# Rope queries of the second four heads made inside the second pair of attention heads, in a two-layer hybrid encoder on one core

## The chip, the cores and the metric

The kernel runs on one core of a Trainium2 chip. The metric is the device time of one execution in microseconds. The engines named below are TensorE (PE, with its weight loads as PEld), VectorE (DVE), ScalarE (ACT), GpSimd (POOL) and SyncE (SP). POOL and SP issue the transfers of this kernel, each in its own order.

## The reference

Two layers work on x, 512 positions by 2048. Each layer makes one wide projection of the normalised x, runs three groups of heads on parts of it, multiplies by a gate, projects back and adds the normalised result to x. The lines that matter here are those of the latent attention (8 heads; each query and key has 128 plain and 64 rotated components) and of the memory attention (4 heads against 256 memory tokens):

```python
q = (rmsnorm(q_lat, q_norm_g[l]) @ w_uq[l]).reshape(b, s, MLA_HEADS, QK_HEAD_DIM)
q = jnp.concatenate([q[..., :QK_NOPE_DIM],
                     apply_rope(q[..., QK_NOPE_DIM:], cos[:, :, None, :], sin[:, :, None, :])], axis=-1)
kv = (rmsnorm(kv_lat, kv_norm_g[l]) @ w_ukv[l]).reshape(b, s, MLA_HEADS, QK_NOPE_DIM + V_HEAD_DIM)
k_nope, v = kv[..., :QK_NOPE_DIM], kv[..., QK_NOPE_DIM:]
a_out = mla_attention(q, k, v)              # softmax(q k^T) v, 8 heads, 512 x 512
mem_n = rmsnorm(mem, mem_norm_g[l])
m_out = memory_attention(q_mem, mem_n, w_mk[l], w_mv[l])   # 4 heads, 512 x 256
y = jnp.concatenate([a_out, c_out, m_out], axis=-1) * jax.nn.silu(gate)
x = x + rmsnorm(y @ w_o[l], post_norm_g[l])
```

`apply_rope` multiplies the 64 components by a table of cosines and sines: with halves a and b it returns a·cos − b·sin and b·cos + a·sin. The queries of all eight heads need it. Here they are made in two halves: the first serves heads 0 to 3, the second heads 4 to 7.

## The kernel before

**Products.** Every fp32 product is three matmuls of a number split in two parts, high and low (`mm3`, lines 267 to 269). A split is a pair of instructions: ACT writes the high part, DVE the rest (`split_to`, lines 272 and 273). Weights come from memory as 128x1024 tiles `wr` in a pool of 8 raw tiles, and are split to `wh` (ACT, line 184) and `wl` (DVE, line 185), in pools of 3 tiles each. Larger things (queries Q, keys K, values V, transposed probabilities PT, the rotated queries QR, the split memory tokens mHL) lie in a pool of 19 slabs of 128x2048. The tile that takes over a slab or a raw tile waits until every reader of the old one is done, a transfer that reads it included.

**The attention part of a layer** is `mixer` (line 1202). It begins with a prelude: the products of the first half of the rope queries (`p0`, 24 matmuls into two PSUM tiles `qr`), the gates, the rotation of the first half, and the products of the second half (`p1`, 24 matmuls more). Then 16 steps follow for the four memory heads (one head, four blocks of 128 queries, scores of 128x256), so m = 16, and 32 steps for the eight latent heads, which are taken in four pairs (pair 0 is heads 0 and 1, steps m to m + 7; pair 1 is heads 2 and 3, steps m + 8 to m + 15). A step puts one block's scores `sc` on PE, and behind it the softmax: the negative row maximum `nm` on DVE (line 1125), the exponential and the scaling `P` on ACT (1128, 1131) with the reciprocal `rec` on DVE (1130). Some steps later the block's probabilities are transposed (`ptp`, line 1141) and split, and the head's output `o` is made from them and V. The scores of a latent head end in two matmuls of rotated parts (lines 1122 and 1123), which read the slab QR: heads 0 to 3 read the first half's, heads 4 to 7 the second half's.

**Work between the steps.** `between` is a table from the step's number to other work that is put behind that step's scores. It holds the steps that make Q, K and V of the next pair (`qkv_steps`, spread over the pair before), the rotation of the second half, and, in layer 0, eight steps that split the memory tokens for layer 1 (`mem_turned_steps`: ACT line 190, DVE line 191, into `mHL`, then transfers to `mTd` in memory by POOL).

**A rotation** has four steps. `first` is one DVE product of 128x1024 with the table `tab` (line 1013), `second` two of 128x512 (1017, 1018), `both` one difference and one sum of 128x512 (1022, 1023), and `away` splits the result into `qrh` and `rm` and writes both to memory with two transfers by POOL (line 1031). `fetch` then reads the result back into QR with four transfers of 256 KB by POOL (line 1036), in which each of four groups of 32 partitions takes one quarter: the first two quarters are the high parts, the last two the low parts.

**What sets the order.** PE, SP and POOL take their instructions in the order in which the program writes them. For DVE and ACT a scheduler chooses the order when the kernel is built, from the same program, and it moves work of the neighbouring steps past each other; on the chip each engine then goes strictly in its order.

Of the kernel before, what the change touches and what calls it, by code (L numbers as in the profile page):

```python
# [82 lines left out]
class Program:  # L83
# [22 lines left out]
    def add(self, fn, units=(), room=0.0, ahead=None):  # L106

        self.steps.append((list(units), fn, room, self.ahead if ahead is None else ahead))
# [114 lines left out]
def encoder(tc, x, xt, mem, memt, positions, columns, w_in, q_norm_g, w_uq, w_qr, kv_norm_g, w_ukv,  # L223
# [4 lines left out]
    depth = w_in.shape[0]  # L228
# [14 lines left out]
    pr = Program(nc, raw_p, hi_p, lo_p)  # L243
# [9 lines left out]
    def bank(name="ps", dt=F32):  # L253
        return banks.tile([P, 512], dt, tag="bank", name=nm(name))

    def slab(name, dt=F32):
        return slabs.tile([P, D], dt, tag="slab", name=nm(name))
# [7 lines left out]
    def mm3(ps, a, b, first, last, **kw):  # L265
        (ah, al), (bh, bl) = a, b
        nc.tensor.matmul(ps, ah, bh, start=first, stop=False, **kw)  # L267
        nc.tensor.matmul(ps, ah, bl, start=False, stop=False, **kw)  # L268
        nc.tensor.matmul(ps, al, bh, start=False, stop=last, **kw)  # L269

    def split_to(hi, lo, src):
        nc.scalar.copy(hi, src)
        nc.vector.tensor_tensor(lo, src, hi.bitcast(F32), op=ALU.subtract)
# [571 lines left out]
    def mem_turned_steps(l):  # L845
        st = {}

        def unit(q):
            def place():
                if q % 2 == 0:  # L850
                    st[q // 2] = slab("mHL", F32R)
                return tuple(st[q // 2][:, o:o + 512] for o in ((q % 2) * 512, 1024 + (q % 2) * 512))
            return Unit(("mT", l, q), {("mT", l, q): [memt[:, 2 * q:2 * q + 2, :]]}, alloc=place,
                        gain=lambda: [G[f"gm_{l}"][:, 2 * q + a:2 * q + a + 1] for a in range(2)])

        def step(q):
            def f(ops):
                if q % 2:
                    c = (q % 4 - 1) * 512
                    for i in range(2):  # L860
                        nc.gpsimd.dma_start(G["mTd"][2 * (q // 4) + i, :, c:c + 1024],
                                            st[q // 2][:, i * 1024:(i + 1) * 1024].bitcast(F32))
            return f
        return [(step(q), [unit(q)]) for q in range(8)]
# [177 lines left out]
    def qkv_steps(l, pair, st):  # L1042
        wl = w_uq[l].rearrange("(a p) (h c) -> p a h c", p=P, c=NOPE + ROPE)
        wkv = w_ukv[l].rearrange("(a p) c -> p a c", p=P)
        qk, kk = ("uq", l, pair), ("ukv", l, pair)
        qu = Unit(qk, {qk: [wl[:, :, 2 * pair + i, :NOPE] for i in range(2)]})
        ku = Unit(kk, {kk: [wkv[:, :, pair * 512:(pair + 1) * 512]]})

        def two(name):
            return slab(name, F32R).rearrange("p (s i c) -> p s i c", s=2, i=2)  # L1050

        def fq(i):
            def g(*ch):
                if ch:
                    st["qw"] = ch[0]
                    st["Q"] = two("Q")
                hi, lo = (a[:, i * 512:(i + 1) * 512].rearrange("p (j c) -> p j c", j=4) for a in st["qw"])
                cH, cL = G["cq"]
                ps = bank("qps")
                for j in range(4):  # L1060
                    mm3(ps, (hi[:, j, :], lo[:, j, :]), (cH[:, j, :], cL[:, j, :]), j == 0, j == 3)
                split_to(st["Q"][:, 0, i, :], st["Q"][:, 1, i, :], ps)
            return g

        def fk(i):
            def g(*ch):
                if ch:
                    st["kw"] = tuple(a.rearrange("p (j c) -> p j c", j=2) for a in ch[0])
                    st["K"] = two("K")
                hi, lo = st["kw"]  # L1070
                cH, cL = G["ckv"]
                ps = bank("kps")
                for j in range(2):
                    mm3(ps, (hi[:, j, i * 256:i * 256 + P], lo[:, j, i * 256:i * 256 + P]),
                        (cH[:, j, :], cL[:, j, :]), j == 0, j == 1)
                split_to(st["K"][:, 0, i, :], st["K"][:, 1, i, :], ps)
            return g

        def fv(b):
            def g():  # L1080
                if b == 0:
                    st["V"] = slab("V", F32R).rearrange("p (s k c) -> p s k c", s=2, k=NT)
                hi, lo = (a.rearrange("p j (h c) -> p j h c", h=2)[:, :, :, NOPE:] for a in st["kw"])
                cH, cL = G["ckv"]
                ps = bank("vps")
                for i in range(2):
                    sl = slice((2 * b + i) * P, (2 * b + i + 1) * P)
                    for j in range(2):
                        mm3(ps[:, i * 256:(i + 1) * 256].rearrange("p (h c) -> p h c", h=2),
                            (cH[:, j, sl], cL[:, j, sl]), (hi[:, j], lo[:, j]), j == 0, j == 1)  # L1090
                p3 = ps.rearrange("p (i c) -> p i c", i=2)
                split_to(st["V"][:, 0, 2 * b:2 * b + 2, :], st["V"][:, 1, 2 * b:2 * b + 2, :], p3)
            return g

        return [(fq(0), [qu]), (fq(1), []), (fk(0), [ku]), (fk(1), []), (fv(0), []), (fv(1), [])]
# [65 lines left out]
    def mla_head(h, st):  # L1161
        i = h % 2

        def src():
            Q, K, V = st["Q"], st["K"], st["V"]
            ds = slice(i * P, (i + 1) * P)
            return (Q[:, 0, i], Q[:, 1, i], K[:, 0, i], K[:, 1, i]), (lambda k: V[:, 0, k, ds], lambda k: V[:, 1, k, ds])
        return head_iters(h, h, src, S, h < HEADS - 1)

    def mem_head(i):  # L1170
        def src():
            Q, K, V = G["Qm"], G["Km"], G["Vm"]
            ds = slice(i * P, (i + 1) * P)
            return ((Q[0][:, i], Q[1][:, i], K[:, 0, i], K[:, 1, i]),
                    (lambda k: V[:, 0, k, ds], lambda k: V[:, 1, k, ds]))
        return head_iters(12 + i, None, src, MT)
# [18 lines left out]
    def spread(n, steps, start=0.0):  # L1195

        out = {}
        for k, s in enumerate(steps):
            out.setdefault(int(n * start + k * n * (1 - start) / len(steps)), []).append(s)
        return out  # L1200

    def mixer(l, C, gates, pair2, tail):

        add(tables_fetch)
        add(mem_fetch)
        gs = [(g, []) for g in gates]
        (p0, rotate0, fetch0), (p1, rotate1, fetch1) = (q_rope_steps(l, g) for g in range(2))
        put(p0[:1], gs[:4], p0[1:])
        put(rotate0, gs[4:], p1)
        sts = [{} for _ in range(4)]  # L1210
        qkv = qkv_steps(l, 0, sts[0])
        qkv[0] += (0.0, 1)
        qkv[2] += (0.0, 0)
        its = [it for i in range(4) for it in mem_head(i)]
        m = len(its)
        between = spread(m, qkv)
        between.setdefault(6, []).append((fetch0, []))
        for k, f in zip((2, 4, 6, m + 2), rotate1):
            between.setdefault(k, []).append(f)
        between.setdefault(m - 3, []).append((lambda: pr.prep_next(), []))  # L1220
        for pair in range(4):
            for i in range(2):
                its += mla_head(2 * pair + i, sts[pair])
            nxt = tail if pair == 3 else spread(6 if pair == 2 else 8, qkv_steps(l, pair + 1, sts[pair + 1]))
            if pair == 2:
                nxt.update(pair2)
            if pair < 2 and l + 1 < depth:
                turned = turned if pair else mem_turned_steps(l + 1)
                for k in range(4):
                    nxt.setdefault(2 * k + 1, []).append(turned[4 * pair + k])  # L1230
            for k, v in nxt.items():
                between.setdefault(m + 8 * pair + k, []).extend(v)
        between.setdefault(m + 9, []).append((fetch1, []))
        pipeline(its, between, m)


# [138 lines left out]
    def put(*passes):  # L1375
        for steps in passes:
            for s in steps:
                add(*s)
# [22 lines left out]
    for l in range(depth):  # L1401
        G["left"] = L = Left(l > 0)
        C, gs, owns = projection(l)
# [151 lines left out]
        if l + 1 < depth:  # L1555
            add(lambda: G.update(mTd=dram.tile([4, P, D], F32, name="mTd")))
        mixer(l, C, gates, {6: [(use_y, []), (low(0), [])], 7: [(low(1), [])]}, last_pair)
        add(sums(1))
        add(gains(0))
# [55 lines left out]
```

## Time and profile before

| | |
|---|---|
| median of 3 runs | 1482.05 us (1480.98 to 1482.29) |
| the profiled execution | 1483.54 us |
| its span, first to last instruction | 1481.8 us |
| busy PE, DVE, ACT, POOL | 99%, 73%, 58%, 18% |
| granted TensorE clock, mean | 0.998 |
| layer 0: prelude's end, memory heads, pair 0 | 447.4 to 453.0, to 478.0, to 507.3 us |
| layer 1: memory heads, pair 0, pair 1 | 1186.2 to 1211.0, to 1240.0, to 1269.0 us |

A row of a timeline gives the start, the length, the engine, the line, what is written and read, and in brackets the idle time before it and what ended it. A row of a window gives its length and then, for PE, PEld, DVE, ACT and POOL in this order, the busy time with the number of instructions, and at last the granted clock, the transfers' share and GB/s. Matmuls are pipelined: a 128x512 matmul has a row of 0.39 us, but in an unbroken run such matmuls start 0.227 us apart, so a pause that is shorter than the difference shows as no idle time.

### The profile page before, as it was taken

How to read it: one execution, taken by the hardware profiler on the slowest of the kernel's cores; microseconds unless marked ns; L12 is line 12 of the kernel's file. 1: busy time of each engine (PE TensorE's matmuls, PEld its weight loads, DVE VectorE, ACT ScalarE, POOL GpSimd, SP SyncE). 2: the span in 40 equal slices, each digit the busy share in tenths (PEclk: the TensorE clock that was granted, in tenths of full speed). 3: DMA queues.
4: the chain of work that ended last, by engine and by line, in shares of the span. 5: the costliest groups of instructions: out<-in, count | busy, mean ns of one | idle time of the engine just before them, and what ended most of it. 6: DMA issues, size and time to landing. Idle time of an engine off the chain costs nothing.

```text
span 1481.8 us, 19603 instructions
## 1 busy us (share of the span) xinstructions
PE 1467.4 (99%) x7267; PEld 1255.2 (85%) x7267; DVE 1087.6 (73%) x1441; ACT 862.7 (58%) x1313; POOL 270.2 (18%) x274
## 2 busy tenths in 40 slices
PE   9999999999999999999999999999999999999997
PEld 9887888899888888888898888888988888888886
DVE  5799677857567768869789666776575576688687
ACT  6856343446458878654677534434464587786443
POOL 0022302031300200220220333030322010003111
PEclk9999999999999999999999999999999999999999
DMA  9999978697964732595986999696979563028945
GB/s 366 399 250 206 221 197 186 169 189 216 211 193 100 230 134 72 115 212 163 346 291 226 239 228 221 197 176 160 211 196 216 167 151 92 29 86 146 261 119 185
DMA packets 142192, 287.88 MB, mean 194 GB/s; under 512 B 9808, under 2 KB 32592, under 8 KB 138256
## 3 DMA queue, kind: packets, MB, share of 16 engines
q0 software_dynamic: 56288, 128.47, 42.9%
q1 hardware_dynamic: 85664, 158.11, 32.1%
q8 instruction: 57, 0.93, 0.3%
q14 instruction: 39, 0.32, 0.1%
q10 hardware_dynamic: 144, 0.05, 0.1%
HBM read 264.96 MB, written 21.63 MB: 193 GB/s over the span
## 4 chain that ended last, share of the span: by engine, by line
PE 82%; issue 6%; DMA 5%; ACT 3%; DVE 3%; POOL 1%; POOLq 0%; DVEq 0%; SPq 0%; ACTq 0%
PE P L268 21%; PE P L267 21%; PE P L269 21%; PE ptp L1141 2%; PE o L268 1%; PE o L269 1%; DMA wr<-in_w_mk_dram 1%; POOL wr L142 1%; PE o L267 1%; PE tps L883 1%; DMA X<-in_xt_dram 1%; DMA wr<-in_w_in_dram 1%; PE sc L268 1%; PE sc L267 1%; PE sc L269 1%
## 5 line engine op out<-in xcount | busy, mean ns | idle before, releaser
L184 ACT CAST wh<-wr 128x1024 fp32r<-128x1024 f32 (+2 forms) x433 | 444.6, 1030 | 462.4 <-PE P L269 364.9
L185 DVE TENSOR_TENSOR wl<-wr,wh 128x1024 fp32r<-128x1024 f32 (+2 forms) x433 | 515.8, 1194 | 266.1 <-ACT wh L184 259.2
L267 PE MATMUL P<-wh,S 128*128 128x512 f32 (+1 forms) x896 | 345.2, 385 | 0.0
L268 PE MATMUL P<-wl,S 128*128 128x512 f32 (+1 forms) x896 | 344.0, 384 | 0.3 <-DVE wl L185 0.3
L269 PE MATMUL P<-wh,S 128*128 128x512 f32 (+1 forms) x896 | 343.2, 383 | 0.0
L267 PE MATMUL P<-wh,A 128*128 128x512 f32 (+1 forms) x656 | 253.0, 386 | 0.0
L268 PE MATMUL P<-wl,A 128*128 128x512 f32 (+1 forms) x656 | 251.8, 384 | 0.8 <-DVE wl L185 0.8
L269 PE MATMUL P<-wh,A 128*128 128x512 f32 (+1 forms) x656 | 251.5, 383 | 0.0
L142 POOL DMA_DIRECT2D wr<-in_w_in_dram x132 | 158.9, 1204 | 439.4 <-DVE wl L185 324.9
L268 PEld LDWEIGHTS P<-wl,S 128*128 128x128 f32 x896 | 168.2, 188 | 30.6 <-DVE wl L185 1.3
L269 PEld LDWEIGHTS P<-wh,S 128*128 128x128 f32 x896 | 168.2, 188 | 30.3
L267 PEld LDWEIGHTS P<-wh,S 128*128 128x128 f32 x896 | 168.1, 188 | 29.8
L268 PEld LDWEIGHTS P<-wl,A 128*128 128x128 f32 x656 | 123.2, 188 | 23.0 <-DVE wl L185 1.6
L269 PEld LDWEIGHTS P<-wh,A 128*128 128x128 f32 x656 | 123.1, 188 | 22.4
L267 PEld LDWEIGHTS P<-wh,A 128*128 128x128 f32 x656 | 123.1, 188 | 21.8 <-ACT og L575 0.2
L142 POOL DMA_DIRECT2D wr<-in_w_o_dram x40 | 48.5, 1237 | 350.4 <-DVE wl L185 347.0
L1128 ACT ACTIVATE P<-sc,nm 128x512 f32<-128x512 f32 (+1 forms) x96 | 60.0, 625 | 31.9 <-DVE nm L1125 31.9
L1131 ACT ACTIVATE P<-P,rec 128x512 f32<-128x512 f32 (+1 forms) x96 | 62.3, 662 | 10.0 <-DVE rec L1130 10.0
L1125 DVE TENSOR_REDUCE nm<-sc 128x1 f32<-128x512 f32 (+1 forms) x96 | 56.5, 592 | 7.9 <-PE sc L1123 4.3
L1141 PE MATMUL ptp<-identr,P 128*128 128x128 f32 x320 | 46.1, 273 | 0.1
L173 DVE TENSOR_TENSOR wr<-wr,wr 128x1024 f32<-128x1024 f32 (+1 forms) x36 | 42.4, 1177 | 3.5 <-DMA wr<-in_w_in_dram 2.3
L1141 PEld LDWEIGHTS ptp<-identr,P 128*128 128x128 f32 x320 | 37.8, 140 | 5.9 <-ACT P L1131 0.5
(318 smaller groups left out, 2103.2 us busy)
## 6 DMA issues: line engine op xcount, KB each, us to landing
wr<-in_w_in_dram SPq DMA_DIRECT2D x128, 512.0 KB, 4.9
wr<-in_w_in_dram POOLq DMA_DIRECT2D x108, 512.0 KB, 7.3
wr<-in_w_o_dram SPq DMA_DIRECT2D x48, 512.0 KB, 6.5
wr<-in_w_o_dram POOLq DMA_DIRECT2D x40, 512.0 KB, 6.8
wr<-in_w_in_dram SPq DMA_DIRECT2D x32, 416.0 KB, 3.8
wr<-in_w_in_dram POOLq DMA_DIRECT2D x24, 416.0 KB, 5.7
wr<-in_w_mk_dram SPq DMA_DIRECT2D x16, 512.0 KB, 9.1
wr<-in_w_mv_dram SPq DMA_DIRECT2D x16, 512.0 KB, 10.2
```

The source lines that it names most:

```text
L142: engine.dma_start(dst, src, **kw)
L173: nc.vector.tensor_tensor(tiles[a], tiles[a], tiles[b], op=ALU.add)
L184: nc.scalar.copy(hi[:, h], src[:, h])
L185: nc.vector.tensor_tensor(lo[:, h], src[:, h], hi[:, h].bitcast(F32), op=ALU.subtract)
L267: nc.tensor.matmul(ps, ah, bh, start=first, stop=False, **kw)
L268: nc.tensor.matmul(ps, ah, bl, start=False, stop=False, **kw)
L269: nc.tensor.matmul(ps, al, bh, start=False, stop=last, **kw)
L883: nc.tensor.transpose(ps[:, t * P:(t + 1) * P], view(t)[:, j * P:(j + 1) * P], G["ident"])
L1125: nc.vector.tensor_reduce(nmax, ps, axis=AX.X, op=ALU.max, negate=True)
L1128: nc.scalar.activation(pt, ps, AF.Exp, bias=nmax, accum_out=tot)
L1131: nc.scalar.activation(pt, pt, AF.Copy, scale=rec)
L1141: nc.tensor.transpose(ps[:, k * P:(k + 1) * P], pt[:, k * P:(k + 1) * P], G["ident"])
```

## The change

The products of the second half (`p1`) leave the prelude and stand, twelve matmuls each, at steps m + 7 and m + 8. The four steps of its rotation go from steps 2, 4, 6 and m + 2 to steps m + 9 to m + 12, and the fetch from step m + 9 to m + 14. Because the raw tile of the table is given back in between, the table is fetched a second time in each layer, at step m + 6 (one transfer of 512 KB by POOL). In layer 0 the eight steps on the memory tokens go from steps m + 1, m + 3, ... m + 15 to m + 13 and m + 15 to m + 21. The steps that make pair 1's Q, K and V begin at step m + 2 rather than m, and the preparation of the next weights is asked for at step m, not m − 3.

```diff
-        put(rotate0, gs[4:], p1)
+        put(rotate0, gs[4:])
...
-        for k, f in zip((2, 4, 6, m + 2), rotate1):
-            between.setdefault(k, []).append(f)
-        between.setdefault(m - 3, []).append((lambda: pr.prep_next(), []))
+        between[m] = [(lambda: pr.prep_next(), [])]
...
-            nxt = tail if pair == 3 else spread(6 if pair == 2 else 8, qkv_steps(l, pair + 1, sts[pair + 1]))
+            nxt = tail if pair == 3 else spread(6 if pair == 2 else 8, qkv_steps(l, pair + 1, sts[pair + 1]),
+                                                0.0 if pair else 0.25)
...
-            if pair < 2 and l + 1 < depth:
-                turned = turned if pair else mem_turned_steps(l + 1)
-                for k in range(4):
-                    nxt.setdefault(2 * k + 1, []).append(turned[4 * pair + k])
...
-        between.setdefault(m + 9, []).append((fetch1, []))
+        late = [(7, p1[0]), (8, p1[1])] + list(zip((9, 10, 11, 12), rotate1)) + [(14, (fetch1, []))]
+        late.append((6, (tables_fetch, [])))
+        if l + 1 < depth:
+            late += zip((13, 15, 16, 17, 18, 19, 20, 21), mem_turned_steps(l + 1))
+        for k, s in late:
+            between.setdefault(m + k, []).append(s)
```

The number of PE instructions stays. Three places show the new order.

DVE at the start of the memory heads of layer 0, before: the end of the first half's rotation, and the second half's begun among the first softmax instructions. Numbers behind a name tell one tile from the next; `rm_3917` is the second half's.

```order
L185 TENSOR_TENSOR wl_3818<-wr_3549,wh_3817 128x1024
L273 TENSOR_TENSOR rm_3778<-rm_3778,qrh_3784 128x1024
L1125 TENSOR_REDUCE nm_3851<-sc_3847 128x1
L185 TENSOR_TENSOR wl_4196<-wr_3593,wh_4195 128x1024
L1013 TENSOR_TENSOR rm_3917<-qr_3821,tab_3715 128x1024
L1130 RECIPROCAL rec_3856<-tot_3854 128x1
L273 TENSOR_TENSOR Q_3862<-qps_3863,Q_3862 128x512
L1125 TENSOR_REDUCE nm_3882<-sc_3878 128x1
L1125 TENSOR_REDUCE nm_3894<-sc_3890 128x1
L1017 TENSOR_TENSOR qr_3821<-qr_3834,tab_3715 128x512
```

The same place after:

```order
L1125 TENSOR_REDUCE nm_3820<-sc_3816 128x1
L185 TENSOR_TENSOR wl_4221<-wr_3549,wh_4220 128x1024
L273 TENSOR_TENSOR rm_3779<-rm_3779,qrh_3785 128x1024
L1125 TENSOR_REDUCE nm_3850<-sc_3846 128x1
L1130 RECIPROCAL rec_3825<-tot_3823 128x1
L1125 TENSOR_REDUCE nm_3862<-sc_3858 128x1
L273 TENSOR_TENSOR Q_3830<-qps_3831,Q_3830 128x512
L1130 RECIPROCAL rec_3855<-tot_3853 128x1
L1130 RECIPROCAL rec_3867<-tot_3865 128x1
L1125 TENSOR_REDUCE nm_3889<-sc_3885 128x1
```

The first scores now come ahead of the first half's low part, and no rotation stands among the softmax instructions.

DVE in pair 1 of layer 1, from the product with V of head 1 (`o_11089` after) on. The scores named `sc_11126` before and `sc_11119` after are the same, the first block of head 3. Before:

```order
L1130 RECIPROCAL rec_11093<-tot_11091 128x1
L1156 TENSOR_TENSOR y_10155<-o_11096,y_10155 128x512
L273 TENSOR_TENSOR PTl_11111<-ptp_11112,PTh_11110 128x4x128
L273 TENSOR_TENSOR PTl_11111<-ptp_11119,PTh_11110 128x4x128
L1125 TENSOR_REDUCE nm_11132<-sc_11126 128x1
L1130 RECIPROCAL rec_11137<-tot_11135 128x1
```

and after:

```order
L1022 TENSOR_TENSOR rm_11025<-rm_11025,qr_10983 128x512
L1023 TENSOR_TENSOR rm_11025<-rm_11025,qr_10904 128x512
L1130 RECIPROCAL rec_11084<-tot_11082 128x1
L1156 TENSOR_TENSOR y_10157<-o_11089,y_10157 128x512
L273 TENSOR_TENSOR PTl_11104<-ptp_11105,PTh_11103 128x4x128
L1125 TENSOR_REDUCE nm_11125<-sc_11119 128x1
L273 TENSOR_TENSOR PTl_11104<-ptp_11112,PTh_11103 128x4x128
L273 TENSOR_TENSOR rm_11025<-rm_11025,qrh_11142 128x1024
L1130 RECIPROCAL rec_11130<-tot_11128 128x1
```

The low part of the second half's rotation, which the last two transfers of the fetch need, now stands behind the row maximum of `sc_11119`.

POOL in layer 1, before:

```order
L992 DMA tab_10124<-tabd 128x1024
L875 DMA Km_10126<-Kmd_7283 128x2048
L875 DMA Vm_10128<-Vmd_7243 128x2048
L1031 DMA qrd_0_10197<-qrh_10194 128x2x512
L1031 DMA qrd_0_10197<-rm_10188 128x2x512
L1036 DMA QR_10407<-qrd_0_10197 32x4x512 x4
L1031 DMA qrd_1_10760<-qrh_10757 128x2x512
L1031 DMA qrd_1_10760<-rm_10326 128x2x512
L1036 DMA QR_11033<-qrd_1_10760 32x4x512 x4
```

and after:

```order
L992 DMA tab_10126<-tabd 128x1024
L875 DMA Km_10128<-Kmd_7285 128x2048
L875 DMA Vm_10130<-Vmd_7245 128x2048
L1031 DMA qrd_0_10199<-qrh_10196 128x2x512
L1031 DMA qrd_0_10199<-rm_10190 128x2x512
L1036 DMA QR_10373<-qrd_0_10199 32x4x512 x4
L992 DMA tab_10867<-tabd 128x1024
L1031 DMA qrd_1_11145<-qrh_11142 128x2x512
L1031 DMA qrd_1_11145<-rm_11025 128x2x512
L1036 DMA QR_11221<-qrd_1_11145 32x4x512 x4
```

The second table fetch is new, and the second half's writes and reads follow it directly.

## The prediction

> **What bounds the kernel now.** First the shares of the engines on the profile's page, then what PE waits for, on the same page, and then windows over the stages that the change touches.
>
> ```profile
> span 1481.8 us, 19603 instructions
> PE 1467.4 (99%) x7267; PEld 1255.2 (85%) x7267; DVE 1087.6 (73%) x1441; ACT 862.7 (58%) x1313; POOL 270.2 (18%) x274
> ```
>
> PE is busy for 1467.4 of 1481.8 us and its instructions stay the same, so only PE's pauses can be won, and a new pause is paid in full. The windows (PE, PEld, DVE, ACT, POOL in this order) are the prelude's last piece with the products to be moved, the memory heads and pair 0 of layer 0, then memory heads and pair 1 of layer 1:
>
> ```profile
> 447.40:453.00 5.60, 5.60 (x27) 4.66 (x26) 3.45 (x4) 2.43 (x4) 1.41 (x2) 1.00 0.11 42
> 453.00:478.00 25.00, 24.21 (x164) 21.68 (x164) 21.40 (x55) 22.36 (x64) 2.28 (x5) 1.00 0.65 138
> 478.00:507.30 29.30, 28.36 (x156) 23.82 (x155) 23.18 (x50) 24.94 (x58) 3.65 (x6) 1.00 0.61 208
> 1186.20:1211.00 24.80, 23.92 (x162) 21.43 (x161) 21.16 (x54) 22.08 (x63) 2.25 (x5) 1.00 0.75 160
> 1240.00:1269.00 29.00, 29.00 (x158) 24.86 (x157) 18.49 (x34) 20.41 (x41) 0.00 (x0) 1.00 0.27 55
> ```
>
> PE stands idle for 0.79 us in the memory heads of layer 0, 0.88 in those of layer 1, and 0.94 in pair 0 of layer 0. In pair 1 of layer 1 it never does. Where it does, the timelines of DVE and PE say why. Memory heads of layer 0, DVE and then PE:
>
> ```profile
> 466.50 1.22 DVE L185 TENSOR_TENSOR wl<-wr,wh 128x1024 fp32r<-128x1024 f32 x1
> 467.64 0.42 DVE L273 TENSOR_TENSOR PT<-ptp,PT 128x256 fp32r<-128x256 f32 x1
> 467.97 0.15 DVE L1130 RECIPROCAL rec<-tot 128x1 f32<-128x1 f32 x1
> 468.04 0.40 DVE L273 TENSOR_TENSOR PT<-ptp,PT 128x256 fp32r<-128x256 f32 x1
> ```
>
> ```profile
> 468.11 0.38 PE L268 MATMUL o<-PT,Vm 128*128 128x256 f32 x1 [0.71 <-DVE PT L273]
> ```
>
> DVE is packed there, and the low part of the transposed probabilities comes after a weight split. In pair 0 of layer 0 it is something else, a slab (DVE, then PE):
>
> ```profile
> 493.44 0.87 DVE L191 SCALAR_TENSOR_TENSOR mHL<-wr,cols,mHL 128x256 fp32r<-128x256 f32 x2
> 496.81 0.69 DVE L273 TENSOR_TENSOR PTl<-ptp,PTh 128x512 fp32r<-128x512 f32 x1 [2.50 <-DMA mTd<-mHL]
> ```
>
> ```profile
> 503.74 0.49 PE L267 MATMUL o<-PTh,V 128*128 128x512 f32 x1 [0.50 <-ACT PTh L272]
> 504.67 0.50 PE L268 MATMUL o<-PTl,V 128*128 128x512 f32 x1 [0.44 <-DVE PTl L273]
> ```
>
> The new PTl takes a slab from which mHL is still being written to memory; DVE stands still for 2.50 us, and both splits are late when PE wants them. A matmul of 128x512 has a row of 0.39 us but a pitch of 0.227 us, so each pause costs up to 0.16 us more than its idle time.
>
> **The change part by part.**
>
> *The moved products.* 24 matmuls at 0.227 us are 5.45 us of PE in either place: nothing by themselves. In the prelude they cover the end of the first rotation (DVE 3.45 us, ACT 2.43 us in the first window). That cover goes; the first scores then meet DVE at its weight split, about 1 us later relative to PE than now.
>
> *The rotation leaves the memory heads.* Its rows on DVE are one of 128x1024 and four of 128x512; the latter follow each other at a pitch of 0.59 us (459.60 to 460.19):
>
> ```profile
> 456.21 1.23 DVE L1013 TENSOR_TENSOR rm<-qr,tab 128x1024 f32<-128x1024 f32 x1 [0.89 <-DMA qrd<-rm]
> 459.60 0.68 DVE L1018 TENSOR_TENSOR qr<-qr,tab 128x512 f32<-128x512 f32 x1
> 460.19 0.68 DVE L1023 TENSOR_TENSOR rm<-rm,qr 128x512 f32<-128x512 f32 x1
> ```
>
> That is 1.23 + 4 x 0.59 = 3.6 us of DVE out of 21.40, and its wait of 0.89 us too. PE's pauses there are between 0.79 us (idle rows) and, where the matmuls' starts are spaced too wide at four places with 0.16 to 0.25 us hidden in each, some 1.8 us. The gain lies between 0, if the lost cover takes all of it back, and 1.8. More than half of the jam goes, and the later start eats part: I take −1.1 in layer 0 and −1.0 in layer 1.
>
> *The memory tokens leave pair 0 of layer 0.* No mHL stands before PTl there any more. The gain is 0.94 (idle) to 1.4 us (with what the two rows hide); nothing in the order then follows on the same slabs within pair 0, so I take −1.4. The eight steps land in pairs 1 and 2. In the two busiest of the windows above, DVE works 23.18 of 29.3 us with part of them; the DVE of a pair without any is at 18.49 of 29.0, like pair 1 of layer 1, and four steps there are about 4 us (eight instructions at 0.44, from the pair of 0.87). They fit beside PE: 0, and at worst one pause of the kind of 0.94.
>
> *The second table fetch.* One transfer of 512 KB, issued at step m + 6, wanted at m + 9. Three steps are some 10 us (a pair of eight is 29). No transfer of this kind beside such work is in the trace; the nearest rows are below and land in 3.5 to 11.1 us, so 0 to about 1 us, on DVE and not on PE: 0.
>
> *The fetch of the second half in layer 0.* The low part stands three steps earlier on DVE there than in layer 1, and the four reads have most of head 2's and head 3's steps to land: 0, and a pause of 1 to 2 us if they take the longest time below.
>
> *The same fetch in layer 1.* Here the change puts a wait in front of PE. In the new order DVE makes the low part of the rotation behind the row maximum of head 3's first block. PE's order from that block to head 4's first rotated matmul is the old one, so the old timeline gives the time that is left:
>
> ```profile
> 1256.69 0.39 PE L1123 MATMUL sc<-KAB,QR 128*128 128x512 f32 x1
> 1269.76 0.39 PE L1122 MATMUL sc<-KAB,QR 128*128 128x512 f32 x1
> ```
>
> The block is done at 1256.69 + 0.39 = 1257.08, and QR is wanted at 1269.76. Between them stand, on DVE, the maximum and a PTl (0.6 us each, by the pitch of such rows above), and then the low part. Its row, and the transfers behind it, from the first half's rotation in both layers:
>
> ```profile
> 450.74 1.23 DVE L273 TENSOR_TENSOR rm<-rm,qrh 128x1024 fp32r<-128x1024 f32 x1 [1.11 <-ACT qrh L272]
> ```
>
> ```profile
> 452.33 0.74 POOL L1031 DMA_DIRECT2D qrd<-rm  x1 [0.47 <-DVE rm L273]
> ...
> 456.41 1.08 POOL L1036 DMA_DIRECT2D QR<-qrd  x2 [0.31 <-DMA qrd<-rm]
> ```
>
> ```profile
> 1185.50 0.74 POOL L1031 DMA_DIRECT2D qrd<-rm  x1 [0.47 <-DVE rm L273]
> ...
> 1189.90 1.08 POOL L1036 DMA_DIRECT2D QR<-qrd  x2 [0.66 <-DMA qrd<-rm]
> ```
>
> The low part ends at 1257.1 + 0.6 + 0.6 + 1.2 = 1259.5. POOL issues its write 0.36 later (451.97 to 452.33): 1259.9. The read of the third quarter starts 4.08 or 4.40 us after that, when the write has landed, and the fourth 0.54 behind it: at 1264.65. How long a quarter then takes, from issue to landing, the four fetches of the trace say (least, median, most of four; layer 0's first and second half, then layer 1's):
>
> ```profile
> DMA to landing us min/median/max: 4.6/7.2/9.1
> ```
>
> ```profile
> DMA to landing us min/median/max: 6.0/9.0/11.1
> ```
>
> ```profile
> DMA to landing us min/median/max: 6.6/9.4/10.1
> ```
>
> ```profile
> DMA to landing us min/median/max: 3.5/4.5/6.1
> ```
>
> The wait is 1264.65 + landing − 1269.76 = landing − 5.1: none at 3.5, 1.0 us at 6.1, 4.0 at 9.1, 5.0 at 10.1, 6.0 at 11.1. The quietest row (6.1) read while nothing else was loaded; here two raw tiles fall free as the writes land, and weights of 512 KB each are loaded beside it. The two rows that were issued as this will be, two and two with a write between, are 9.1 and 10.1: I take 9.6, a wait of 4.5 us. Before, the same read was issued 33 us ahead of its use:
>
> ```profile
> 1236.42 2.20 POOL L1036 DMA_DIRECT2D QR<-qrd  x4 [17.97 <-PE sc L269]
> ```
>
> PE's queue stops with the rotated matmul; the softmax of head 4 and the products for pair 3 stand behind it, so nothing is made up.
>
> *The sum.* −1.1 − 1.4 − 1.0 + 4.5 = +1.0 us. The profiled execution took 1483.54 us (1.74 around its span) and would take 1484.5; it lay 1.5 above the median, 1482.05, which goes to 1483.05.
>
> [...]
>
> **The rivals.**
>
> *No wait in layer 1.* The last quarter lands within 5.1 us. For it: one fetch's median was 4.5, its least 3.5, and only two quarters are left by then. Against it: the last quarter was the slowest or near it, and none of the four fetches was done in 5.1. It gives −3.5 at no wait and −2.5 at 1.0 us: 1478.55 to 1479.55. Chance 0.13.
>
> *Slower, by a clock that falls.* The wait itself can cost more than its length. After the last matmul the granted clock halves (windows, then PE's last row):
>
> ```profile
> 1470.00:1474.00 4.00, 3.40 (x15) 2.47 (x14) 2.83 (x5) 0.51 (x2) 0.65 (x1) 1.00 0.31 122
> 1474.00:1478.00 4.00, 0.00 (x0) 0.00 (x0) 3.55 (x6) 0.18 (x2) 0.54 (x1) 0.83 0.67 256
> 1478.00:1481.80 3.80, 0.00 (x0) 0.00 (x0) 0.00 (x0) 0.00 (x0) 0.00 (x0) 0.50 0.46 155
> ```
>
> ```profile
> 1473.01 0.39 PE L269 MATMUL P<-T4h,A 128*128 128x512 f32 x1
> ```
>
> A mean of 0.83 over 4 us, full first and half then, is a fall at 1476.6, 3.2 us after that matmul. A wait of 3.2 us or more in layer 1 could do the same, and each 2 us at half clock lose 1. How long it stays low the trace does not show; if as long as it took to fall, 3 to 4 us, the price is 2 us: 1485.05, slower than the bound. The place is head 4's first rotated matmul, the point from which it decides a wait of 3.2 us. Against it: one fall is all that there is to go by, and it may need more idle time than that. Chance 0.12. [...]
>
> *Slower, by a fetch that takes longer than any of the four.* 12 us or more, a wait above 6.9, a sum above +3.4: 1485.4 and up. The weights beside it speak for it; the longest of sixteen quarters, 11.1, against it. With it I count a jam in pairs 1 and 2, where DVE gets 3.6 + 1.2 us more beside 18.49 of 29.0, and a late fetch in layer 0: each costs 1 to 3 us. Chance 0.17.
>
> **How the numbers follow.** The likeliest case is a wait between 1.0 and 6.0 us in layer 1, sums of −2.5 to +2.5, with 0.58: the median at 1483.05, its own range 1479.55 to 1484.55. A change of 0.2%, 2.96 us, is about what a measurement of this kernel tells from none, so this case is "the same". The first rival is faster where the gain passes 2.96, most of its 0.13: I put 0.12 on faster, the rest to the same, 0.59. Clock and long fetch give slower, 0.29. The range, 1479.1 to 1486.6, leaves out the best half of the first rival and the worst of the last.
>
> **What would show it.** Right: in pair 0 of layer 0 no wait of DVE for mTd and no idle row of PE near its product with V; in the memory heads no 0.7 us row. In layer 1, at head 4's first block, the rotated matmul idle for some 4.5 us, released by the transfer into QR, with weights landing beside. The first two right and no wait at QR: the first rival. A granted clock under 1.00 just behind the wait: the second. Wrong altogether would be a pause that moved to another place: in pair 1 behind the rotation on DVE, at the fetch in layer 0, or in the memory heads, where the lost cover may cost more than the rotation gave.

## The result, and the profile after

| | before | after |
|---|---|---|
| median | 1481.80 us (1480.98 to 1482.91, 6 runs) | 1486.93 us (1485.86 to 1488.38, 6 runs) |
| the profiled execution, and its span | 1483.54, 1481.8 us | 1486.93, 1485.1 us |
| busy PE, start of the last matmul | 1467.4, at 1473.01 us | 1467.0, at 1476.43 us |

The changed kernel is slower: the ratio is 1.0034, with a 95% interval of 1.0023 to 1.0045, or 5.1 us between the medians. The two profiled executions lie only 3.4 us apart, since that of before was 1.7 us above its median and that of after on it.

What PE waited for, by the profile of after (us in total, times, longest):

```profile
PE sc L1122 <- DMA QR<-qrd: 5.3, 1, 5.3
...
PE ptp L1141 <- ACT P L1131: 0.8, 2, 0.4
```

The two lines of before on the memory heads and pair 0 (1.4 us for the low part of PT, 0.5 us for PTh) are gone, and one wait of 5.3 us has come. The same view of before had:

```profile
PE o L268 <- DVE PT L273: 1.4, 2, 0.7
...
PE o L267 <- ACT PTh L272: 0.5, 1, 0.5
```

PE's timeline of after shows it in layer 1, at head 4's first score block:

```profile
1265.83 0.40 PE L269 MATMUL sc<-K,Q 128*128 128x512 f32 x1
1271.57 0.76 PE L1122 MATMUL sc<-KAB,QR 128*128 128x512 f32 x1 [5.34 <-DMA QR<-qrd]
1272.13 0.63 PE L1123 MATMUL sc<-KAB,QR 128*128 128x512 f32 x1
1272.56 0.63 PE L267 MATMUL qps<-cqH,wh 128*128 128x512 f32 x1
```

From 1265.83 to 1271.57 there are 5.74 us where 0.23 are usual: a wait of 5.51 us. Behind it the rows are 0.63 us long and start 0.43 us apart, nearly twice the pitch of 0.227. The windows of after (PE, PEld, DVE, ACT, POOL, then the granted clock, the transfers' share and GB/s) say why:

```profile
1267.00:1269.00 2.00, 0.00 (x0) 0.00 (x0) 0.14 (x1) 0.00 (x0) 0.00 (x0) 1.00 1.57 178
1269.00:1271.00 2.00, 0.00 (x0) 0.00 (x0) 0.00 (x0) 0.00 (x0) 0.00 (x0) 0.99 1.13 242
1271.00:1273.00 2.00, 1.43 (x4) 1.17 (x5) 0.20 (x1) 0.00 (x0) 0.00 (x0) 0.50 0.13 47
1273.00:1275.00 2.00, 2.00 (x7) 1.60 (x6) 0.65 (x2) 1.25 (x3) 0.00 (x0) 0.66 0.03 8
1275.00:1277.00 2.00, 2.00 (x10) 1.61 (x9) 0.00 (x0) 0.84 (x2) 0.00 (x0) 1.00 0.00 0
```

The clock fell to half just before the transfer landed (0.99 is 0.04 us of half clock at the end of that window) and came back at about 1274.36 (a mean of 0.66 is 1.36 us at half). The seven starts behind QR's, from 1272.13 to 1274.56, are late by another 1.4 us together.

The chain that leads to it, DVE and then POOL of after, and the landing of the four reads:

```profile
1253.42 0.69 DVE L1125 TENSOR_REDUCE nm<-sc 128x1 f32<-128x512 f32 x1 [0.28 <-PE sc L1123]
1254.03 0.68 DVE L273 TENSOR_TENSOR PTl<-ptp,PTh 128x512 fp32r<-128x512 f32 x1
1254.63 1.22 DVE L273 TENSOR_TENSOR rm<-rm,qrh 128x1024 fp32r<-128x1024 f32 x1
```

```profile
1256.23 0.74 POOL L1031 DMA_DIRECT2D qrd<-rm  x1 [0.64 <-DVE rec L1130]
1258.61 1.12 POOL L1036 DMA_DIRECT2D QR<-qrd  x2 [1.64 <-PE ptp L1141]
1260.57 1.08 POOL L1036 DMA_DIRECT2D QR<-qrd  x2 [0.84 <-DMA qrd<-rm]
...
DMA to landing us min/median/max: 6.2/8.8/10.4
```

The fourth read goes out at 1261.1 and lands 10.4 us later, at 1271.5. QR had been wanted at 1265.83 + 0.23 = 1266.06. Meanwhile SP issues three weight loads of 512 KB (1258.11 is the start of the first; the second starts at 1260.06). Below the row stands what SP's queue waited for in that stretch, from 1257 to 1266 us (us in total, times, longest): the landing of the rotation's two writes, at 1258.05 and 1260.04. The third load waits for DVE.

```profile
1258.11 6.80 SPq L142 DMA_DIRECT2D wr<-in_w_o_dram  x3
```

```profile
SPq L142 <- DMA qrd<-qrh: 12.1, 1, 12.1
...
SPq L142 <- DMA qrd<-rm: 1.6, 1, 1.6
```

The gains are there too. By the spacing of matmul starts, PE's pauses in the memory heads of layer 0 fell from 1.6 to 0.8 us, in those of layer 1 from 1.7 to 0.8, and in pair 0 of layer 0 from 1.4 to 0, where DVE no longer waits for `mTd`. That is −3.1 us; the wait and the half clock are +6.9. The two last matmuls start 3.4 us apart; the −0.4 us that remain are −0.75 from the first 400 us, ahead of all that was changed, and some +0.35 spread over the rest.

### The profile page after: what moved, and what is told of

It is laid out like the page before. It is cut to its first block, busy times and chain, and to the rows that moved or that the text cites. A ratio compares the mean times of both kernels' runs of the same rounds, so it can differ in the third digit from the quotient of the medians.

```text
span 1485.1 us, 19604 instructions
## 1 busy us (share of the span) xinstructions
PE 1467.0 (99%) x7267; PEld 1255.8 (85%) x7267; DVE 1087.4 (73%) x1441; ACT 862.5 (58%) x1313; POOL 270.1 (18%) x276
## 4 chain that ended last, share of the span: by engine, by line
PE 85%; DMA 5%; ACT 3%; DVE 3%; issue 2%; POOL 0%; SPq 0%; POOLq 0%; DVEq 0%; ACTq 0%
PE P L267 22%; PE P L268 22%; PE P L269 22%; PE ptp L1141 2%; PE tps L883 2%; DMA wr<-in_w_mv_dram 2%; DMA wr<-in_w_in_dram 1%; PE o L268 1%; PE o L269 1%; PE o L267 1%; DVE wl L185 1%; PE sc L268 1%; PE sc L267 1%; PE sc L269 1%; DMA wr<-in_w_mk_dram 1%
## 6 DMA issues: line engine op xcount, KB each, us to landing
wr<-in_w_mv_dram SPq DMA_DIRECT2D x16, 512.0 KB, 10.8
```

## The experiments

All kernels are the changed one with the edit shown, unless said otherwise. Ratios are to the kernel before, timed beside them on the same chip.

**Layer 1 as before, layer 0 as changed.**

```diff
-        put(rotate0, gs[4:])
+        put(rotate0, gs[4:], p1 if l else [])
...
-        between[m] = [(lambda: pr.prep_next(), [])]
+        if l:
+            for k, f in zip((2, 4, 6, m + 2), rotate1):
+                between.setdefault(k, []).append(f)
+        between.setdefault(m - 3 if l else m, []).append((lambda: pr.prep_next(), []))
...
+        late = [(9, (fetch1, []))] if l else (
+            [(7, p1[0]), (8, p1[1])] + list(zip((9, 10, 11, 12), rotate1)) + [(14, (fetch1, []))])
+        if not l:
+            late.append((6, (tables_fetch, [])))
```

Pair 1's steps start at step m again in layer 1.

> Layer 0 as changed, layer 1 as before. Theory A (the loss is the late fetch in layer 1 and the half clock behind it, some 6.9 us; the rest of the change gains some 3.3): no wait of PE for QR, the 0.73 us row in layer 1's memory heads back, 2.3 us faster than before (0.9 from the memory heads and 1.4 from pair 0 of layer 0), ratio 0.9984. Rival B (the rest of the change gains nothing in the median either): ratio 1.000 or above.

Measured: 1481.54 us, ratio 0.9992 (0.9983 to 1.0001). No wait for QR and no wide row is left. In layer 1 PE's trace has the old pause again:

```profile
1199.42 0.39 PE L268 MATMUL o<-PT,Vm 128*128 128x256 f32 x1 [0.73 <-DVE PT L273]
```

So the loss sits in layer 1 alone. The gain expected from layer 0, 0.9984, is inside the interval, near its edge; in PE's starts between 400 and 640 us the trace shows 2.1 us less than before.

**One step earlier, and three steps earlier.**

```diff
-        late = [(7, p1[0]), (8, p1[1])] + list(zip((9, 10, 11, 12), rotate1)) + [(14, (fetch1, []))]
-        late.append((6, (tables_fetch, [])))
+        late = [(6, p1[0]), (7, p1[1])] + list(zip((8, 9, 10, 11), rotate1)) + [(13, (fetch1, []))]
+        late.append((5, (tables_fetch, [])))
```

Three steps earlier all these numbers are smaller by 2 more.

> Products, rotation, table and fetch of the second half one step earlier in both layers. By the orders the low part then has 17.6 us of PE work ahead of its use in layer 1, not 12.9. Theory A: the wait of 5.5 us shrinks by those 4.8 to some 0.7 us, the clock stays at 1.00, 2.6 us faster than before, ratio 0.9982. Rival (the landing is set by the weight loads beside it, and moves with them): a wait of 2 us or more stays.

> The same three steps earlier, 24.9 us of PE work ahead of the use. Theory A: no wait for QR at all, 3.3 us faster than before, ratio 0.9978. Rival (the rotation now jams DVE at the end of pair 0, where the probabilities are split): new idle rows of PE of 0.5 to 1 us there, ratio 0.9985 or above, and not better than one step earlier.

Measured: one step earlier 1481.33 us, ratio 0.9990 (0.9982 to 0.9999); three steps 1480.25 us, ratio 0.9982 (0.9974 to 0.9991). With one step the wait is down to one row of PE, 0.47 us wide of its place by the starts, and the clock stays at 1.00 (another row of 0.47 us stands at layer 0's read):

```profile
1267.44 0.47 PE L1122 MATMUL sc<-KAB,QR 128*128 128x512 f32 x1 [0.30 <-issue]
```

With three steps it is gone, and there is no new pause at pair 0's end. The reads themselves land no sooner (one step, then three):

```profile
DMA to landing us min/median/max: 6.2/8.5/10.1
```

```profile
DMA to landing us min/median/max: 8.4/9.9/11.9
```

In both kernels the first two weight loads go out less than 0.1 us behind the landing of the rotation's two writes, so the loads move with the rotation, as the rival had it. The wait of 2 us or more that the rival expected did not come: the wait shrinks because the chain starts earlier against its use.

**Matmuls in the gap.** Matmuls on the identity, whose result nobody reads, stand in layer 1 behind the last score block of head 3, so that PE comes to the rotated matmul later and idles less in front of it: 44 of them, then 32, then 20. What is computed otherwise stays.

```diff
+    def fill(n):
+        ps = bank("warm")
+        for k in range(n):
+            nc.tensor.matmul(ps[:, (k % 4) * P:(k % 4 + 1) * P], G["identr"], G["identr"], start=True, stop=True)
...
+        if l:
+            late.append((15, (lambda: fill(44), [])))
```

> The change, with 44 matmuls on the identity (128x128, some 5.0 us, their result unused) put in layer 1 behind the last score block of head 3. Theory A with the clock: PE waits 0.5 us instead of 5.5 and the clock stays at 1.00, so 1.3 us less than the change, ratio to before 1.0025 with the change's at 1.0034. Rival (the half clock is only how the rows are shown and costs nothing): the same time as the change, and wide rows behind the wait.

> As the filled kernel, but with 20 matmuls on the identity (2.3 us): PE then idles some 3.2 us in front of QR, the same QR time in all. [...] If any idle time of 3 us is enough: wide rows behind the wait and the time of the change, 1.0034.

> As the filled kernel, with 32 matmuls on the identity (3.6 us): PE then idles some 1.9 us in front of QR. With 20 of them and 3.3 us idle the clock fell, with 44 and 0.15 us it did not. [...]

Measured: 1485.46 us and 1.0021 (1.0012 to 1.0030) with 44; 1486.84 us and 1.0024 (1.0014 to 1.0035) with 32; 1488.34 us and 1.0030 (1.0020 to 1.0040) with 20. The last read lands 9.9, 10.8 and 10.5 us behind its issue (10.4 in the change), so with a clock that stays the three would lie within 0.9 us of each other. PE's row at QR, with 44 matmuls, 32 and 20:

```profile
1270.51 0.47 PE L1122 MATMUL sc<-KAB,QR 128*128 128x512 f32 x1
```

```profile
1270.92 0.77 PE L1122 MATMUL sc<-KAB,QR 128*128 128x512 f32 x1 [2.14 <-issue]
```

```profile
1271.32 0.77 PE L1122 MATMUL sc<-KAB,QR 128*128 128x512 f32 x1 [3.13 <-issue]
```

With 44 the clock stays at 1.00, the rows behind are 0.40 us, and the ratio is lower than the change's by 0.0013, 1.9 us, against an expected 1.3; 0.5 us of it is the quicker landing, going by the profiled executions. The intervals of the two ratios overlap; the rows do not. With 32 and 20 the clock fell in the profiled execution (windows of 20 matmuls):

```profile
1268.00:1270.00 2.00, 0.19 (x1) 0.00 (x0) 0.99 (x2) 0.17 (x1) 0.00 (x0) 1.00 1.39 198
1270.00:1272.00 2.00, 0.68 (x2) 0.61 (x3) 0.00 (x0) 0.00 (x0) 0.00 (x0) 0.58 0.55 173
1272.00:1274.00 2.00, 2.00 (x6) 1.54 (x5) 0.69 (x1) 0.72 (x2) 0.00 (x0) 0.50 0.03 8
1274.00:1276.00 2.00, 2.00 (x6) 1.59 (x5) 0.16 (x1) 0.78 (x2) 0.00 (x0) 0.50 0.00 0
1276.00:1278.00 2.00, 2.00 (x8) 1.54 (x7) 0.00 (x0) 0.50 (x1) 0.00 (x0) 0.71 0.00 0
```

0.58, 0.50, 0.50 and 0.71 make it half from 1270.32 to 1277.16. So in these executions pauses of 2.1 and 3.1 us were enough, and with 20 matmuls the wide rows came that were expected if a pause of 3 us is enough. The executions of one kernel differ: with 32 the three quickest, 1484.75 to 1485.96 us, have mean clocks of 0.998 and 0.999, the five others, 1486.52 to 1488.58 us, four times 0.997 and once 0.998. That fits a fall in some executions only; the profiled one, of 1486.52 us, is one in which it fell.

**The tokens alone.** The kernel before, with only the eight steps of layer 0 moved.

```diff
-                for k in range(4):
-                    nxt.setdefault(2 * k + 1, []).append(turned[4 * pair + k])
...
+            for k, s in zip((13, 15, 16, 17, 18, 19, 20, 21), mem_turned_steps(l + 1)):
+                between.setdefault(m + k, []).append(s)
```

> The kernel before with the eight steps on the memory tokens alone moved, as the change moves them. Theory A: the wait of 2.50 us of DVE for mTd in pair 0 of layer 0 and the two idle rows of PE there go, 1.4 us faster, ratio 0.9990; memory heads as before (0.71 and 0.73 us rows). Rival (another tile takes the same place behind a transfer): idle rows of 0.4 to 0.5 us in pair 0 or 1 stay, ratio 1.000.

Measured: 1482.19 us, ratio 0.9992 (0.9983 to 1.0000). From 453 to 510 us the only wait left of PE is that of the memory heads:

```profile
PE o L268 <- DVE PT L273: 0.7, 1, 0.7
```

Pair 0's two are gone, so the term is shown by itself in the trace; in the time it is at the edge of what can be told.

**Why the read lands late: two kernels.** In the first SP issues layer 1's late reads into QR, which puts them ahead of two of the weight loads in SP's order. In the second POOL issues them as in the change, but the rotation's tiles lie in a slab, so that no weight load waits for the rotation's writes.

```diff
-                nc.gpsimd.dma_start(q[i * HALF:(i + 1) * HALF], st["d"][i].rearrange("h i c -> i h c"))
+                (nc.sync if l and g else nc.gpsimd).dma_start(
+                    (lambda v: v.bitcast(F32) if l and g else v)(q[i * HALF:(i + 1) * HALF]), st["d"][i].rearrange("h i c -> i h c"))
```

```diff
+            if l and g:
+                st["rot"] = slab("rot").rearrange("p (h s c) -> p h s c", h=2, s=2)
-            m = st["m"] = halves("rm")
+            m = st["m"] = st["rot"][:, 0] if l and g else halves("rm")
...
-            m, hi = st["m"], halves("qrh", F32R)
+            m, hi = st["m"], st["rot"][:, 1].bitcast(F32R) if l and g else halves("qrh", F32R)
```

> The change with the four reads into QR of layer 1's second half issued by SP instead of POOL, between the same weight loads. If the late landing is the POOL queue's own slowness: landing 4 to 6 us from issue, the wait 1 to 2 us, clock 1.00, ratio 0.999. If it is the weights beside it, the reads land about as late, 9 to 10 us, with a wait of 4 us or more and a ratio of 1.002 or above.

> The change with the tiles of layer 1's second rotation in a slab, not in two raw tiles, so that no weight load waits for the rotation's writes to land and then runs beside the read. If the weights beside it set the landing: the last quarter lands some 6 us after its issue, PE waits about 1 us, clock 1.00, ratio 0.9987. If the queue is slow by itself: landing 9 to 10 us, wait 4 to 5.5 us, ratio 1.002 or above.

Measured: by SP 1479.60 us, ratio 0.9980 (0.9971 to 0.9988); in a slab 1479.90 us, ratio 0.9977 (0.9968 to 0.9986). Neither has a wait at QR. The landing by SP, then with the slab (POOL):

```profile
DMA to landing us min/median/max: 3.6/4.5/5.8
```

```profile
DMA to landing us min/median/max: 3.8/4.6/5.4
```

The second settles it: the same queue, the same four reads, no weights issued between 1249.2 and 1264.4 us (two loads in the row below, the first at its start and the second at its end), and 5.4 us in place of 10.4. POOL's queue is not slow by itself; the weights beside it cost 5 us. With SP the reads also overtake two loads, so that run alone does not tell queue from neighbours.

```profile
1249.17 15.61 SPq L142 DMA_DIRECT2D wr<-in_w_o_dram  x2
```

In the slab kernel the chain started earlier as well:

```profile
1250.33 0.72 POOL L1033 DMA_DIRECT2D qrd<-rot  x1 [42.99 <-ACT rot L272]
1251.93 0.74 POOL L1033 DMA_DIRECT2D qrd<-rot  x1 [0.88 <-DVE rec L1132]
1255.10 1.12 POOL L1038 DMA_DIRECT2D QR<-qrd  x2 [2.43 <-DMA qrd<-rot]
1256.42 1.08 POOL L1038 DMA_DIRECT2D QR<-qrd  x2 [0.20 <-issue]
```

The second pair of reads goes out at 1256.42 rather than 1260.57. With 10.4 us its last would have landed at 1267.4, with QR wanted at 1266.6: the earlier start alone takes most of the wait away, and the quick landing the rest with 4 us to spare. Both kernels are faster than the one before and the changed one.

**The cover.** The slab kernel with the products left in the prelude; only the rotation is late.

```diff
-        put(rotate0, gs[4:])
+        put(rotate0, gs[4:], p1)
...
-        late = [(7, p1[0]), (8, p1[1])] + list(zip((9, 10, 11, 12), rotate1)) + [(14, (fetch1, []))]
+        late = list(zip((9, 10, 11, 12), rotate1)) + [(14, (fetch1, []))]
```

> As the kernel with the rotation in a slab, but with the products of the second half left in the prelude in both layers; only the rotation is late. It prices the cover that the change takes from the memory heads. If the cover is what the two idle rows left there (0.57 and 0.24 us in each layer, from the starts of the matmuls) hang on: both shorter or gone, 0.5 to 1.6 us faster than with the products moved, ratio 0.997. If the two PSUM tiles held through the memory heads cost more: new idle rows there, ratio 0.998 or above.

Measured: 1483.43 us, ratio 1.0006 (0.9998 to 1.0015), some 4 us slower than with the products moved. What PE waits for in the memory heads of layer 0:

```profile
PE kps L267 <- DVE PT L273: 0.4, 1, 0.4
PE kps L267 <- ACT P L1130: 0.4, 1, 0.4
PE o L267 <- ACT P L1130: 0.3, 1, 0.3
```

The expectation of a gain fell, and the second outcome, new idle rows, came. Three starts there are late by 0.49 to 0.57 us each, 1.6 us in all, as much as before the change, and the same three stand in the memory heads of layer 1. With the products moved it is 0.8 us in each layer, so these rows are 1.6 of the some 4 us; what makes up the rest was not traced. That the two PSUM tiles held through the memory heads do this is likely but only argued: the tiles go round among eight, and the waits are those of work that writes a PSUM tile.

## Why the prediction was wrong

The prediction gave 1483.05 us, no measurable change, and a range to 1486.6; 1486.93 came. Taken by its own steps, against the two traces:

| step | predicted | in the trace |
|---|---|---|
| memory heads, layer 0 and 1 | −1.1, −1.0 | −0.8, −0.9 |
| memory tokens out of pair 0 | −1.4 | −1.4 |
| second table, layer 0's fetch, pairs 1 and 2 | 0 | 0, no wait |
| wait for QR in layer 1 | +4.5 | +5.5 |
| half clock behind it | 0 | +1.4 |
| sum | +1.0 | +3.8 |

With these terms as measured the forecast from 1482.05 would have been 1485.85, inside the range. No trace places the 1.1 us from there to 1486.93; the six executions of the kernel before spread over 1.9 us, those of the changed one over 2.5.

The mechanism was right to the place. The low part behind the row maximum of head 3's first block, the write 0.36 us after it (0.38), the read 4.08 to 4.40 us after that (4.34), and a wait of the landing less 5.1 us: with the measured 10.4 this gives 5.3, and 5.5 was seen.

Two terms failed. The landing was taken as 9.6 us, between the two rows that were issued alike; it was 10.4, and 9.9 to 10.8 in the three kernels with matmuls in the gap, beside the same weight loads. That is one of the terms mis-sized, by 0.8 us of landing; the wait came out 1.0 us longer than the forecast.

The other is a fault of reasoning. I put the fall of the clock in a rival with a chance of 0.12, with a wait of 3.2 us as the point from which it decides, and forecast a wait of 4.5 us, which is past that point. The likeliest case had to hold the price it set off. Counted, with the 2 us given there, the sum is +3.0: slower. The price was 1.4 us by the starts, one stay of 3.4 us at half clock. The ground for doubt, that one fall at the end of the run was all there was to go by, was a reason for a wider range and not for leaving the term out.

The memory heads gained 0.4 us less in all: the lost cover left rows of 0.57 and 0.24 us, where 0.65 was assumed in total.

Of the rivals, "no wait" needed a landing of 5.1 us. The slab kernel came to 5.4 with no weights beside it, so what spoke for it was a quiet queue, and the change itself takes the quiet away: its rotation tiles are raw tiles, and each write that lands hands one to a weight load. Two readings of the prediction were wrong there without moving its sum. Its quietest fetch, with 6.1 us for the last quarter, was not alone: in the trace of before a weight load starts at 1238.87, 0.8 us behind the last read. And of that rival's 0.13 it put 0.12 on faster, though by its own sum the gain passes 2.96 only for a wait under 0.54 us, about half of the rival.

## What to carry to other kernels

A step that is moved late has to be timed as a chain to its first use, and each transfer in it priced beside the loads that the move itself sets free; a tile that comes from another pool can keep those loads away. A pause on PE need not be paid in its own length alone: here pauses of 2.1 us and more brought a stretch at half clock in the profiled executions, and those of 0.7 us in the memory heads before did not. Put the price of that stretch into the forecast, not beside it. If a late chain has a few steps of slack, starting it one to three steps earlier keeps the gain, as 0.9990 and 0.9982 show against 1.0034.

## What the runs showed of the hardware

With 32 and with 20 matmuls in the gap the clock fell 2.1 us after the last matmul was done (at 1270.88 and 1270.32, with the last matmul done at 1268.78 and 1268.19), at the end of the kernel before 3.2 us after it, and in the change only 4.7 us after it (at 1270.96, with the last matmul done at 1266.23): the idle time ahead of the fall was not the same in these executions. What sets it was not shown.

Worked out from the means of the windows, the clock then stayed at half for 3.40 us in the change, for 3.40 us with 32 matmuls (means of 0.72, 0.50 and 0.93 from 1270 to 1276), and for 6.84 us with 20. So a pause of 2.14 us on PE, with 32 matmuls, brought 3.40 us at half clock, and one of 3.13 us, with 20, brought 6.84; the pause of 0.30 us, one step earlier, brought none. What ends the half clock was not shown.
